# The end of a transformer layer: scattered parts added at once, the norm's gain multiplied in early, and its mean and bias added by two-row matrix products

## The chip, the core and the metric

The kernel runs on one core of one Trainium2 chip. The core has a matrix engine (TensorE, PE in the profile; its weight loads are listed as PEld), a vector engine (VectorE, DVE), an activation engine (ScalarE, ACT), a general engine (GpSimd, POOL) and an engine that only issues transfers (SyncE, SP). ACT can issue transfers as well. Sixteen DMA engines carry all transfers. The metric is the device time of one execution, in microseconds (us).

## What is computed

The reference is one layer of a diffusion transformer on 512 latent tokens of width 1024. The end of it is what matters here: a mixture of 16 experts, of which each takes its 64 best tokens, and then a layer norm.

```python
def ec_moe(h, w_router, b_router, w1, w3, w2):
    cap = EC_CAPACITY * n // N_EXPERTS                 # 64
    aff = softmax(h @ w_router + b_router)
    g, idx = lax.top_k(swapaxes(aff, 1, 2), cap)
    xe = h[bidx, idx]
    hid = silu(xe @ w1) * (xe @ w3)                    # per expert
    ye = (hid @ w2) * g[..., None]
    return zeros_like(h).at[bidx, idx].add(ye)

x = layer_norm(ALPHA * x + g2 * ec_moe(x * (1 + sc2) + sh2, *moe), ln2_g, ln2_b)

def layer_norm(x, g, b):
    return (x - mean(x)) * rsqrt(var(x) + EPS) * g + b
```

All arithmetic is float32. The weights w1, w3 and w2 of the sixteen experts are 201 MB and are read once.

## The kernel before

**Stages.** The first half of the kernel is attention and is untouched. From about 600 us on the experts run in eight pairs (`for pr in range(E_N // 2)`, L1232). The tokens are kept as four tiles of 128 rows, `xn[0]` to `xn[3]` (normalized input) and `acc[0]` to `acc[3]` (the running sum, four tiles of 128x1024).

**One pair.** `gather` builds 0/1 rows (`oh`) and multiplies them with `xn` on TensorE (L1137), which picks the 128 tokens of the pair. `up_` multiplies with w1 and w3 (L1174), `hid_t` transposes the result (L1182, copied by ACT in L1183), `down` multiplies with w2 (L1190), and `scatter` scales, splits into a high and a low part and adds the rows back into `acc` through TensorE (L1203, L1204). `gather` for pair 7, the last reader of `xn`, runs inside pair 6, between the two `hid_t` of that pair.

**Weights.** Each piece of 512 KB (`piece`, L957) is loaded by SP into a ring of 36 pages just ahead of its use. SP's instructions run in order. Each transfer from SP or ACT also takes one of eight completion semaphores in turn, and waits until the transfer that had it last has landed.

**The last pair.** Its w2 is cut by columns into three parts (`PARTS`, L40: columns 0 to 383, 384 to 767, 768 to 1023), in 16 pieces of 384 KB and 4 of 512 KB. L1308 multiplies a part into `py`; `put` then scales it (L1283, DVE), splits it (L74 on ACT, the high part; L77 on DVE, the low part), and its `rest` adds it back: for each row tile two products of TensorE (L1291), the addition on DVE (L1295) and the norm's statistics in blocks of 128 columns (L1297). For the third part the sum stays in PSUM (`fin[t]`, started by L1276 with `acc` itself). The code calls `rest` of a part only after the first pieces of the next one (L1310), so that TensorE multiplies while DVE and ACT split.

**The norm.** DVE merges the statistics (L1320), POOL adds epsilon and takes the power -0.5 (L1321, L1322), DVE makes minus mean times factor (L1323). Columns 768 to 1023 go ACT (L1325, from PSUM), POOL times gain (L1329), POOL plus bias (L1330), out. Columns 0 to 767 take two DVE instructions per row tile: (x - mean) times gain (L1335), times factor plus bias (L1336), out (L1337). The gain and bias, each spread over 128 partitions (512 KB), are loaded by SP behind the last weights (L1265).

**Order.** TensorE's instructions stay in written order (`manual_schedule`); a scheduler orders the others engine by engine.

Of the kernel before, what the change touches and what calls it, by code (L numbers as in the profile page):

```python
# [18 lines left out]
D = 1024  # L19
# [10 lines left out]
E_N = 16  # L30
# [21 lines left out]
def _layer(tc, A, out, opened):  # L52
# [1179 lines left out]
    for pr in range(E_N // 2):  # L1232
# [25 lines left out]
        waiting = py, ohT, gt  # L1258


    prefetch(len(order_r))
    ln2 = []
    for nm, place in (("ln2_g", "xe"), ("ln2_b", "hid")):
        b = me.tile([128, D], F32, name="ln2", tag=place, bufs=1)
        dma(b, A[nm].to_broadcast([128, D]))  # L1265
        ln2.append(b)
    lng, lnb = ln2
# [10 lines left out]
    def put(q, py):  # L1278
# [7 lines left out]
        def rest():  # L1286
            for t in range(NT):
# [8 lines left out]
                for b in range(0, w, BN_W):  # L1296
                    V.bn_stats(bs[:, t, (c0 + b) // BN_W, :], r[:, b:b + BN_W])  # L1297
        return rest

    rest = None  # L1300
    for q, (c0, w, ks) in enumerate(PARTS):
        py = psd.tile([128, 512], F32, name="y", bufs=2)
        for kh in range(KD // ks):
# [6 lines left out]
            if rest:  # L1310
                rest()
                rest = None
        rest = put(q, py)
    rest()
    order_.close()
    ov = out[0].rearrange("(t p) d -> p t d", p=128)
    mv = me.tile([128, NT, 2], F32, name="mv2")
    rs2 = me.tile([128, 2, NT], F32, name="rs2")
    for t in range(NT):
        V.bn_aggr(mv[:, t, :], bs[:, t])  # L1320
    G.tensor_scalar(rs2[:, 0, :], mv[:, :, 1], 1.0, EPS / ALPHA ** 2, op0=OP.mult, op1=OP.add)  # L1321
# [60 lines left out]
```

## Time and profile before

| | |
|---|---|
| median of 3 runs | 1049.84 us (1048.28 to 1052.63) |
| the profiled execution | 1047.56 us, of which the span is 1045.8 us |
| mean granted TensorE clock | 0.981 of full |
| TensorE, DVE, ACT, POOL busy | 977.7, 451.9, 278.2, 176.1 us (93, 43, 27, 17%) |
| chain that ended last | PE 72%, DMA 16%, DVE 7%, ACT 2%, issue 2%, POOL 2% |
| read from and written to HBM | 261.47 MB and 2.10 MB |

All times inside the kernel are from the start of the span. Busy shares are averages over a long first half that does not change; what the end of the layer is worth has to be read in the stretch from about 940 us on. A matrix product of float32 shows as two records of TensorE, and TensorE's busy time is modelled where products are pipelined.

### The profile page before, as it was taken

To read this page: it belongs to the slowest core of one execution; us is meant where nothing else is said; L and a number is where in the kernel's file an instruction comes from. 1 tells how busy PE (TensorE), PEld (TensorE's weight loads), DVE (VectorE), ACT (ScalarE), POOL (GpSimd) and SP (SyncE) were. 2 spreads that over 40 slices of the span, in tenths; PEclk is the share of its full clock that TensorE was granted. 3 is DMA by queue.
4 is the path that set the end of the run, shared out by engine and by line. 5 is a ranking of instruction groups with operands and counts; after the bars stand their busy time and mean duration, and the time that the engine had idled before them with its cause. 6 is when DMAs were issued, how large, how long until landed. Compare 5 with 4: busy or idle time off the path is not lost.

```text
span 1045.8 us, 13799 instructions
## 1 busy us (share of the span) xinstructions
PE 977.7 (93%) x5266; PEld 614.1 (59%) x5266; DVE 451.9 (43%) x870; ACT 278.2 (27%) x556; POOL 176.1 (17%) x177
## 2 busy tenths in 40 slices
PE   6999998989999999999986999999999999999992
PEld 5888976768778777777754443535353534334331
DVE  2382365753678556648473512221313131111227
ACT  1222324224777555544120101010101010010010
POOL 2340020202577422210020500000000000000004
PEclk9999999999999999999997999999999999999996
DMA  9944347763012000028948979999999999999993
GB/s 297 290 152 136 97 115 247 232 201 82 21 39 58 22 19 22 21 82 295 411 167 321 371 300 409 409 409 409 409 410 409 408 410 407 410 409 409 409 372 115
DMA packets 101209, 266.97 MB, mean 255 GB/s; under 512 B 14020, under 2 KB 37528, under 8 KB 101144
## 3 DMA queue, kind: packets, MB, share of 16 engines
q1 hardware_dynamic: 100248, 264.52, 68.3%
q0 software_dynamic: 320, 1.05, 0.4%
q8 instruction: 41, 0.67, 0.3%
q10 hardware_dynamic: 576, 0.52, 0.1%
q14 instruction: 24, 0.20, 0.1%
HBM read 261.47 MB, written 2.10 MB: 252 GB/s over the span
## 4 chain that ended last, share of the span: by engine, by line
PE 72%; DMA 16%; DVE 7%; ACT 2%; issue 2%; POOL 2%; SPq 0%; DVEq 0%; ACTq 0%; POOLq 0%
PE h L1174 16%; DMA wr<-moe_w 10%; PE y L1190 9%; PE mx L1137 6%; PE acc L83 5%; PE acc L82 5%; PE acc L81 5%; PE sc L652 4%; PE tpb L660 3%; DMA wa<-w_ada 3%; PE av L840 3%; PE mx L1203 2%; DMA wraw<-w_in 2%; PE tp L236 2%; PE po L83 1%
## 5 line engine op out<-in xcount | busy, mean ns | idle before, releaser
L1174 PE MATMUL h<-wr,xe 128*64 128x512 f32 x1024 | 233.6, 598 | 8.7 <-DMA wr<-moe_w 7.2
L1174 PEld LDWEIGHTS h<-wr,xe 128*64 128x64 f32 x1024 | 68.3, 136 | 162.9 <-issue 106.6
L1190 PE MATMUL y<-wr,hidT 128*64 128x512 f32 x448 | 97.7, 594 | 0.0
L641 DVE TENSOR_REDUCE nm<-sc 128x1 f32<-128x768 f32 x64 | 61.0, 953 | 34.3 <-PE sc L652 33.8
L1177 DVE TENSOR_TENSOR hid<-hid,h 128x512 f32<-128x512 f32 x16 | 11.0, 687 | 145.2 <-PE h L1174 145.2
L1149 POOL TENSOR_TENSOR oh<-oh,aff 128x512 f32<-128x512 f32 x8 | 8.4, 1048 | 352.8 <-PE mx L1137 352.8
L1190 PEld LDWEIGHTS y<-wr,hidT 128*64 128x64 f32 x448 | 31.5, 137 | 61.8 <-issue 58.1
L642 ACT ACTIVATE P<-sc,nm 128x768 f32<-128x768 f32 x64 | 57.6, 901 | 31.8 <-DVE nm L641 22.7
L1137 PE MATMUL mx<-oh,xn 128*128 128x128 f32 x512 | 60.3, 279 | 1.4 <-DVE oh L1127 1.4
L1137 PEld LDWEIGHTS mx<-oh,xn 128*128 128x128 f32 x512 | 59.2, 196 | 2.5 <-issue 1.3
L74 ACT ACTIVATE whi<-wraw 128x1024 fp32r<-128x1024 f32 (+1 forms) x32 | 33.5, 1046 | 99.4 <-DMA wraw<-w_in 75.4
L77 DVE TENSOR_TENSOR wlo<-wraw,whi 128x1024 fp32r<-128x1024 f32 (+1 forms) x32 | 39.2, 1227 | 45.2 <-PE acc L82 29.7
L74 ACT ACTIVATE ye<-y 128x512 fp32r<-128x512 f32 (+2 forms) x17 | 9.7, 572 | 178.8 <-DVE y L1197 98.7
L81 PE MATMUL acc<-xlh,whi 128*128 128x512 f32 x128 | 51.5, 402 | 2.1 <-ACT whi L74 2.1
L1204 DVE TENSOR_TENSOR acc<-acc,mx 128x512 f32<-128x512 f32 x56 | 34.7, 680 | 41.4 <-PE mx L1203 41.4
L1176 ACT ACTIVATE hid<-h 128x512 f32<-128x512 f32 x16 | 9.6, 597 | 155.6 <-PE h L1174 155.6
L82 PE MATMUL acc<-xll,whi 128*128 128x512 f32 x128 | 50.7, 396 | 0.0
L83 PE MATMUL acc<-xlh,wlo 128*128 128x512 f32 x128 | 50.2, 401 | 0.3 <-DVE wlo L77 0.3
L81 PE MATMUL acc<-whi,xlh 128*128 128x512 f32 (+1 forms) x128 | 49.6, 391 | 1.0 <-ACT whi L74 1.0
L1197 DVE SCALAR_TENSOR_TENSOR y<-y,gate,g2b 128x512 f32<-128x512 f32 x14 | 9.9, 754 | 92.5 <-PE y L1190 92.5
L83 PE MATMUL acc<-whi,xll 128*128 128x512 f32 (+1 forms) x128 | 48.7, 381 | 0.5 <-POOL xll L77 0.5
L82 PE MATMUL acc<-wlo,xlh 128*128 128x512 f32 (+1 forms) x128 | 48.8, 381 | 0.2 <-DVE wlo L77 0.2
(339 smaller groups left out, 1707.3 us busy)
## 6 DMA issues: line engine op xcount, KB each, us to landing
wr<-moe_w SPq DMA_DIRECT2D x372, 512.0 KB, 10.2
wa<-w_ada SPq DMA_DIRECT2D x32, 512.0 KB, 4.3
wraw<-w_in SPq DMA_DIRECT2D x28, 512.0 KB, 5.2
wa<-w_ada SPq DMA_DIRECT2D x8, 1024.0 KB, 9.4
wr<-moe_w SPq DMA_DIRECT2D x16, 384.0 KB, 8.5
outraw<-w_out SPq DMA_DIRECT2D x8, 512.0 KB, 9.6
xq<-x SPq DMA_DIRECT2D x4, 512.0 KB, 8.2
q<-q SPq DMA_DIRECT2D x16, 128.0 KB, 2.3
```

Of the source, the lines that this page charges most:

```text
L74: S.activation(hi, src, AF.Copy)
L77: (eng_lo or V).tensor_tensor(lo, src, f(hi), op=OP.subtract)
L81: T.matmul(ps, lh, rh, start=start, stop=False)
L82: T.matmul(ps, lh, rl, start=False, stop=False)
L83: T.matmul(ps, ll, rh, start=False, stop=stop)
L641: V.tensor_reduce(nm, ps[:, :768], axis=AX.X, op=OP.max, negate=True)
L642: S.activation(p, ps[:, :768], AF.Exp, bias=nm, accum_out=z)
L652: T.matmul(ps[:, a:b], l, r[:, a:b], start=i == 0, stop=i == len(passes) - 1)
L1137: T.matmul(pss[hf][:, kk * 128:(kk + 1) * 128], xn[t][:, k * 128:(k + 1) * 128], o[:, t].rearrange("p e s -> p (e s)"), start=t == 0, stop ...
L1174: T.matmul(ph[i][64 * hf:64 * hf + 64, :], xe[:, k, sl], w[:, hf * 512:(hf + 1) * 512], start=k == 0, stop=k == KD - 1)
L1190: T.matmul(py[hf][r0:r0 + 64, :], hT[:, e % 2, fc % 4, fc // 4, :], w[:, hf * 512:(hf + 1) * 512], start=fc == 0, stop=fc == KD - 1)
L1204: V.tensor_tensor(acc[t][:, hs], acc[t][:, hs], ps, op=OP.add)
```

## The change

- The gain and bias rows are loaded by ACT at the end of pair 6, into tiles of `xn` that have no reader any more: the two spread copies of 512 KB (into `xn[1]`, `xn[2]`), and both as two single rows of 4 KB (`gbr`, in `xn[0]`).
- `rest` of a part follows its `put` at once; nothing of the next part stands between.
- After the statistics of parts 0 and 1, each row tile is multiplied by the gain in place, by DVE for part 0 and POOL for part 1.
- Epsilon is added by DVE instead of POOL.
- Minus mean times factor and a column of ones (`mrs`) are transposed by TensorE (four small products into one PSUM tile), copied by DVE into a tile of two rows (`mr`), and multiplied with the gain and bias rows: the product is (-mean x factor) x gain + bias for a whole row tile, 512 and 256 columns at a time.
- Columns 0 to 767 then take one DVE instruction per product: x times factor plus the product, read from PSUM. The last row tile goes out in two transfers, the others in one.

```diff
+        if pr == E_N // 2 - 2:
+            lng, lnb, gbr = xn[1], xn[2], xn[0][0:2]
+            for i, nm in enumerate(("ln2_g", "ln2_b")):
+                S.dma_start(xn[1 + i], A[nm].to_broadcast([128, D]))
+                S.dma_start(xn[0][i:i + 1], A[nm])
...
-    for nm, place in (("ln2_g", "xe"), ("ln2_b", "hid")):
-        b = me.tile([128, D], F32, name="ln2", tag=place, bufs=1)
-        dma(b, A[nm].to_broadcast([128, D]))
...
                 for b in range(0, w, BN_W):
                     V.bn_stats(bs[:, t, (c0 + b) // BN_W, :], r[:, b:b + BN_W])
+                if not last:
+                    (G if q else V).tensor_tensor(r, r, lng[:, qs_], op=OP.mult)
...
-            if rest:
-                rest()
-                rest = None
-        rest = put(q, py)
-    rest()
+        put(q, py)()
...
-    G.tensor_scalar(rs2[:, 0, :], mv[:, :, 1], 1.0, EPS / ALPHA ** 2, op0=OP.mult, op1=OP.add)
-    G.tensor_tensor(rs2[:, 0, :], rs2[:, 0, :], negh[:, :NT], op=OP.pow)
-    V.scalar_tensor_tensor(rs2[:, 1, :], mv[:, :, 0], -1.0, rs2[:, 0, :], op0=OP.mult, op1=OP.mult)
+    V.tensor_scalar(rs2, mv[:, :, 1], EPS / ALPHA ** 2, None, op0=OP.add)
+    G.tensor_tensor(rs2, rs2, negh[:, :NT], op=OP.pow)
+    V.scalar_tensor_tensor(mrs[:, :, 0], mv[:, :, 0], -1.0, rs2, op0=OP.mult, op1=OP.mult)
+    mt = psd.tile([128, 512], F32, name="mx", bufs=3)
     for t in range(NT):
-        S.activation(acc[t][:, c0:], fin[t], AF.Identity, scale=rs2[:, 0, t:t + 1], bias=rs2[:, 1, t:t + 1])
+        T.transpose(mt[0:2, t * 128:(t + 1) * 128], mrs[:, t, :], ident)
+    mr = me.tile([2, 512], F32, name="mr", tag="hid", bufs=1)
+    V.tensor_copy(mr, mt[0:2])
+    for t in range(NT):
+        S.activation(acc[t][:, c0:], fin[t], AF.Identity, scale=rs2[:, t:t + 1], bias=mrs[:, t, 0:1])
+        G.tensor_tensor(acc[t][:, c0:], acc[t][:, c0:], lng[:, c0:], op=OP.mult)
+        G.tensor_tensor(acc[t][:, c0:], acc[t][:, c0:], lnb[:, c0:], op=OP.add)
+        S.dma_start(ov[:, t, c0:], acc[t][:, c0:])
     for t in range(NT):
         o = acc[t]
-        G.tensor_tensor(o[:, c0:], o[:, c0:], lng[:, c0:], op=OP.mult)
-        G.tensor_tensor(o[:, c0:], o[:, c0:], lnb[:, c0:], op=OP.add)
-        S.dma_start(ov[:, t, c0:], o[:, c0:])
-        parts = [slice(0, c0)] if t < NT - 1 else [slice(0, c0 // 2), slice(c0 // 2, c0)]
-        for p in parts:
-            V.scalar_tensor_tensor(o[:, p], o[:, p], mv[:, t, 0:1], lng[:, p], op0=OP.subtract, op1=OP.mult)
-            V.scalar_tensor_tensor(o[:, p], o[:, p], rs2[:, 0, t:t + 1], lnb[:, p], op0=OP.mult, op1=OP.add)
-            dma(ov[:, t, p], o[:, p])
+        for a, b in ((0, 512), (512, c0)):
+            w = psd.tile([128, 512], F32, name="y" if a else "mx", bufs=2 if a else 3)
+            T.matmul(w[:, :b - a], mr[:, t * 128:(t + 1) * 128], gbr[:, a:b], start=True, stop=True)
+            V.scalar_tensor_tensor(o[:, a:b], o[:, a:b], rs2[:, t:t + 1], w[:, :b - a], op0=OP.mult, op1=OP.add)
+            if t == NT - 1:
+                dma(ov[:, t, a:b], o[:, a:b])
+        if t < NT - 1:
+            dma(ov[:, t, :c0], o[:, :c0])
```

On ACT, at the end of pair 6 (`xn_4497` to `xn_4499` are `xn[0]` to `xn[2]`), the order before (-) and now (+) is:

```order
 L1176 ACTIVATE hid<-h 128x512
-L1183 ACTIVATE hidT<-mx 128x512 x2
+L1183 ACTIVATE hidT<-mx 128x512
+L1264 DMA xn_4497<-ln_g 1x1024
+L1183 ACTIVATE hidT<-mx 128x512
+L1263 DMA xn_4498<-ln_g 128x1024
+L1263 DMA xn_4499<-ln_b 128x1024
+L1264 DMA xn_4497<-ln_b 1x1024
 L74 ACTIVATE ye<-y 128x512 x2
```

The four loads stand there in the middle of the weights of the last two pairs; one of them stands ahead of the second copy of `hidT`.

On TensorE, in the last pair (L1308 has become L1311), the order before is:

```order
L1308 MATMUL y<-wr,hidT 64x384 x20
L1291 MATMUL mx<-ye,ohT 128x384 x8
L1308 MATMUL y<-wr,hidT 64x384 x12
L1308 MATMUL y<-wr,hidT 64x256 x8
L1291 MATMUL mx<-ye,ohT 128x384 x8
L1308 MATMUL y<-wr,hidT 64x256 x8
L1291 MATMUL h<-ye,ohT 128x256 x6
L1291 MATMUL mx<-ye,ohT 128x256 x2
```

and now, with the first of the four repeated groups at the end:

```order
L1311 MATMUL y<-wr,hidT 64x384 x16
L1291 MATMUL mx<-ye,ohT 128x384 x8
L1311 MATMUL y<-wr,hidT 64x384 x16
L1291 MATMUL mx<-ye,ohT 128x384 x8
L1311 MATMUL y<-wr,hidT 64x256 x16
L1291 MATMUL h<-ye,ohT 128x256 x6
L1291 MATMUL mx<-ye,ohT 128x256 x2
L1325 MATMUL mx<-ident,mrs 2x128 x4
L1338 MATMUL mx<-xn_4497,mr 128x512
L1338 MATMUL y<-xn_4497,mr 128x256
```

Each adding back now comes directly behind its own part, and twelve products follow where TensorE had nothing left.

On ACT, at the very end, the order before and now (L1325 has become L1330, L1331 has become L1333) is:

```order
-L1325 ACTIVATE acc<-h,rs_7704 128x256 x3
-L1325 ACTIVATE acc<-mx,rs_7704 128x256
-L1331 DMA out<-acc 128x256 x4
+L1330 ACTIVATE acc<-h,mrs,rs_7713 128x256 x3
+L1333 DMA out<-acc 128x256 x3
+L1330 ACTIVATE acc<-mx,mrs,rs_7713 128x256
+L1333 DMA out<-acc 128x256
```

The fourth ACTIVATE, which reads `fin[3]` and frees its PSUM tile, stands now behind three transfers that go out.

## Rows read from the trace of the kernel before

**Rows 1.** Windows: stretch, length, busy PE PEld DVE ACT POOL, clock, DMA share, GB/s.

```profile
760.00:800.00 40.00, 40.00 (x218) 18.94 (x216) 8.60 (x17) 2.99 (x5) 1.05 (x1) 1.00 1.03 409
...
1024.00:1026.00 2.00, 0.80 (x8) 0.27 (x4) 1.89 (x8) 0.01 (x1) 0.00 (x0) 1.00 0.00 0
```

**Rows 2.** Timeline, TensorE, pair 7: start, length, instructions, idle before, releaser.

```profile
989.69 1.08 PE L1174 MATMUL h<-wr,xe 128*64 128x512 f32 x4 [0.20 <-DMA wr<-moe_w]
```

**Rows 3.** DMA issues from 980 us: count, size, median us to landing.

```profile
wr<-moe_w SPq DMA_DIRECT2D x11, 512.0 KB, 10.2
...
ln<-ln_g SPq DMA_DIRECT2D x1, 512.0 KB, 8.7
```

**Rows 4.** Chain that ended last, two pieces near the end: start, length, what.

```profile
1009.41 9.24 DMA wr<-moe_w
...
1041.72 0.96 DVE acc L1336
```

**Rows 5.** Timeline, the last pair's parts, TensorE, DVE and ACT.

```profile
1007.28 0.51 PEld L1308 LDWEIGHTS y<-wr,hidT 128*64 128x64 f32 x5 [0.32 <-DMA wr<-moe_w]
...
1008.83 0.62 DVE L1283 SCALAR_TENSOR_TENSOR y<-y,gate,g2b 128x384 f32<-128x384 f32 x1 [8.30 <-PE y L1308]
...
1010.07 0.56 DVE L77 TENSOR_TENSOR ye<-y,ye 128x384 fp32r<-128x384 f32 x1 [0.62 <-ACT ye L74]
...
1010.83 0.98 PE L1291 MATMUL mx<-ye,ohT 128*128 128x384 f32 x4
...
1012.42 1.25 DVE L1297 BATCH_NORM_STATS2 oh<-acc 128x6 f32<-128x128 f32 x6
...
1013.11 4.85 PE L1308 MATMUL y<-wr,hidT 128*64 128x384 f32 x26
...
1022.85 1.95 PE L1308 MATMUL y<-wr,hidT 128*64 128x256 f32 x16
```

**Rows 6.** Timeline, the tail behind the last part.

```profile
1025.42 0.47 DVE L1283 SCALAR_TENSOR_TENSOR y<-y,gate,g2b 128x256 f32<-128x256 f32 x1
...
1028.90 1.04 DVE L1320 BATCH_NORM_AGGREGATE mv<-oh 128x2 f32<-128x48 f32 x4
...
1030.04 0.83 POOL L1321 TENSOR_SCALAR rs<-mv 128x4 f32<-128x4 f32 x1 [82.79 <-DVE mv L1320]
1030.95 1.04 POOL L1322 TENSOR_TENSOR rs<-rs,negh 128x4 f32<-128x4 f32 x1
1032.03 0.16 DVE L1323 SCALAR_TENSOR_TENSOR rs<-mv,rs 128x4 f32<-128x4 f32 x1 [1.22 <-POOL rs L1322]
```

**Rows 7.** Timeline, a form (busy, mean ns), one line (min/median/max ns): like operations.

```profile
999.66 0.66 PE L1182 MATMUL mx<-ident,hid 128*128 128x128 f32 x4
...
1001.08 1.46 PE L1276 MATMUL h<-acc,ident 128*128 128x256 f32 x6
...
L1308 PE MATMUL y<-wr,hidT 128*64 128x384 f32 x64 | 11.9, 493 | 0.2 <-DMA wr<-moe_w 0.2
...
L1197 DVE SCALAR_TENSOR_TENSOR y<-y,gate,g2b x14: 749/754/759, 621.7 to 961.1; 128x512 f32<-128x512 f32 x14
```

**Rows 8.** Timeline: POOL beside DVE that reads PSUM, and beside the tail's DVE.

```profile
141.49 5.73 POOL L315 TENSOR_TENSOR dq<-rt,rt 128x256 f32<-128x256 f32 x8 [13.02 <-DVE rt L312]
...
1036.57 1.32 POOL L1330 TENSOR_TENSOR acc<-acc,ln 128x256 f32<-128x256 f32 x1
```

**Rows 9.** Windows: length, PE busy, clock, DMA share, GB/s; the last as in Rows 1.

```profile
176.50:177.00 0.50, 0.50 (x2) 0.50 0.00 0
...
179.50:180.00 0.50, 0.50 (x5) 0.99 0.73 107
...
212.00:212.50 0.50, 0.00 (x0) 1.00 0.43 172
...
213.50:214.00 0.50, 0.50 (x4) 0.65 0.72 213
...
1029.25:1029.50 0.25, 0.00 (x0) 0.00 (x0) 0.25 (x3) 0.00 (x0) 0.00 (x0) 0.86 0.00 0
```

More of the change, by code (lines that the diff above doesn't have):

```diff
@@ L1258, in _layer @@
         waiting = py, ohT, gt
-    prefetch(len(order_r))
-    ln2 = []
-    for nm, place in (("ln2_g", "xe"), ("ln2_b", "hid")):
-        b = me.tile([128, D], F32, name="ln2", tag=place, bufs=1)
-        dma(b, A[nm].to_broadcast([128, D]))
-        ln2.append(b)
-    lng, lnb = ln2
+        if pr == E_N // 2 - 2:
[3 more added lines that the diff above has]
+                S.dma_start(xn[0][i:i + 1], A[nm])
+    prefetch(len(order_r))
     nb = D // BN_W
@@ L1297, in rest @@
                     V.bn_stats(bs[:, t, (c0 + b) // BN_W, :], r[:, b:b + BN_W])
-        return rest
-    rest = None
+                if not last:
+                    (G if q else V).tensor_tensor(r, r, lng[:, qs_], op=OP.mult)
+        return rest
+    mrs = me.tile([128, NT, 2], F32, name="mrs")
+    V.memset(mrs[:, :, 1], 1.0)
     for q, (c0, w, ks) in enumerate(PARTS):
@@ L1309, in _layer @@
                              start=fc == 0, stop=fc == KD - 1)
-            if rest:
-                rest()
-                rest = None
-        rest = put(q, py)
-    rest()
-    order_.close()
+        put(q, py)()
     ov = out[0].rearrange("(t p) d -> p t d", p=128)
     mv = me.tile([128, NT, 2], F32, name="mv2")
-    rs2 = me.tile([128, 2, NT], F32, name="rs2")
+    rs2 = me.tile([128, NT], F32, name="rs2")
     for t in range(NT):
         V.bn_aggr(mv[:, t, :], bs[:, t])
-    G.tensor_scalar(rs2[:, 0, :], mv[:, :, 1], 1.0, EPS / ALPHA ** 2, op0=OP.mult, op1=OP.add)
@@ L1326, in _layer @@
-    done = []
+        T.transpose(mt[0:2, t * 128:(t + 1) * 128], mrs[:, t, :], ident)
[6 more added lines that the diff above has]
+        S.dma_start(ov[:, t, c0:], acc[t][:, c0:])
@@ L1327, in _layer @@
     for t in range(NT):
         o = acc[t]
-        G.tensor_tensor(o[:, c0:], o[:, c0:], lng[:, c0:], op=OP.mult)
-        G.tensor_tensor(o[:, c0:], o[:, c0:], lnb[:, c0:], op=OP.add)
-        S.dma_start(ov[:, t, c0:], o[:, c0:])
-        parts = [slice(0, c0)] if t < NT - 1 else [slice(0, c0 // 2), slice(c0 // 2, c0)]
-        for p in parts:
-            with tc.issue_after(done[-1].ins) if t > 1 else nullcontext():
-                V.scalar_tensor_tensor(o[:, p], o[:, p], mv[:, t, 0:1], lng[:, p], op0=OP.subtract, op1=OP.mult)
-            done.append(V.scalar_tensor_tensor(o[:, p], o[:, p], rs2[:, 0, t:t + 1], lnb[:, p], op0=OP.mult, op1=OP.add))
-            dma(ov[:, t, p], o[:, p])
+        for a, b in ((0, 512), (512, c0)):
[4 more added lines that the diff above has]
+                dma(ov[:, t, a:b], o[:, a:b])
@@ L1340 @@
+        if t < NT - 1:
+            dma(ov[:, t, :c0], o[:, :c0])
+    order_.close()
 _INS = ["x", "c", "ctx", "c_ctx", "w_ada", "b_ada", "w_in", "mla_g_q", "mla_w_uq", "mla_g_kv", "mla_w_ukv",
```

## The prediction

> **What bounds the kernel now.** I read the windows first. From 640 us on the sixteen DMA engines are busy all the time and deliver 409 GB/s; nothing moves any more from 1024 us [rows 1]. So the experts run at the pace of their weights. The timeline says the same from TensorE's side: in pair 7 it works 1.08 us and then waits 0.20 us for the next piece [rows 2], and a piece of 0.524 MB takes 1.28 us at 409 GB/s. In the chain of waits the weights hold the end until 1018.65 us (1009.41 + 9.24) [rows 4]. Then a different stage begins: add part 2 back, norm, write. It runs from the scaling of part 2, at 1025.42 us [rows 6], to the end of the span at 1045.8 us, 20.4 us, and DVE is last (1041.72 + 0.96 = 1042.68 us [rows 4]), 3.1 us before the end. So there are three terms: A, what delays the weights; B, the way from part 0's scaling to part 2's; C, these 20.4 us.
>
> **A, the loads.** Two transfers of 0.524 MB leave a place behind the last weights, where they cost nothing: the one of the gain took 8.7 us to land in a queue that had only weights ahead of it [rows 3], and the norm that needs it came later. Now they stand among the weights of pairs 6 and 7, and there the engines have no gap [rows 1]. 1.049 MB at 409 GB/s is 2.56 us, by which every later weight lands later. TensorE is ahead of the weights (0.20 us per piece), so it passes the delay on: up to part 0 all shifts by 2.6 us. Bounds: 0, if the stream had room that the share does not show, and 2.6, since they are the same bytes.
>
> The waits that come with it: ACT's first load waits for the end of `gather` in pair 6. Behind it on ACT stands the second copy of `hidT`, which needs products that come after the same `gather`, so nothing is lost. SP shares the eight semaphores with these loads, and its transfers queue behind a load that is still out; with transfers that take 10.2 us to land at 1.28 us a piece [rows 3], eight are under way, which feeds the engines for some 10 us, and the loads' own bytes for 2.6 more. SP would have to be held longer than that. I take no gap.
>
> **B, adding back at once.** From L1283 of part 0 to the low part is 1.80 us (1008.83 to 1010.63) [rows 5]. Adding back takes 2.28 us from its first product at 1010.83 to the next part's first at 1013.11 [rows 5], of which the first 0.28 is the high part, which now starts before the low one is ready. So part 1 starts 1.80 + 2.0 = 3.8 us after L1283. It has 16 pairs of records; 13 pairs took 4.85 us [rows 5], in which the length of the last record, 0.49 [rows 7], counts once: 0.33 a pair, and 16 pairs with that end 5.4 to 5.8; I take 5.4, since the 13 had a wait at their end. Part 2's eight pairs took 1.95 [rows 5]; with an end of 0.4 that is 0.2 a pair and 3.6 for 16. Sum from L1283 of part 0 to that of part 2: 3.8 + 5.4 + 3.8 + 3.6 = 16.6 us, and 0.1 for the two steps to DVE; before it was 1025.42 - 1008.83 = 16.6. **B is 0.1.** What TensorE lost before in waits for weights (0.32 us at 1007.28 [rows 5], and more at the start of part 2) it now loses in waits for DVE and ACT, and since part 0 was finished by its last weight, A passes through whole. DVE has 12 statistics there at 0.21 and four additions, and now four multiplications, at no more than L77's 0.56 [rows 5]: 7.0 us at most. From the first product put back to part 1's scaling lie 3.8 - 1.8 + 5.4 = 7.4, so they are hidden, though barely; what they need beyond that would make part 1's scaling late by as much. POOL's four, about 1.1 each by the columns of [rows 8], lie in time in which it is idle. The fill of `mrs` and the two small rows are there long before they are read.
>
> Each adding back leaves TensorE idle for 1.24 us (1008.83 to 1010.07 [rows 5]), with small gaps after. The clock can fall in such a place: it was 1.00 at 212.00 us, with TensorE idle, and 0.65, on its way to 0.50, at 213.50 when TensorE worked again [rows 9]. It did not fall when TensorE stopped at 1024.80 [rows 5] for the wait behind part 2 [rows 1]. I take no fall; each would cost some 1.5 us (half of a stretch at 1.2 GHz like that from 176.50 to 179.50 [rows 9]), so B reaches from -0.5 (DVE, busy with part 1, held part 2's scaling by about that before) to 3.1.
>
> **C, the tail, counted from L1283 of part 2.** The merged statistics end at +4.5 as before (1028.90 + 1.04) [rows 6]. Epsilon on DVE costs 0.16, by L1323, plus a step, instead of POOL's 0.83 and its step; the power keeps its 1.04 [rows 6]. So the factor is there 0.75 us earlier, and the transposes start at +6.1. What comes next is new:
>
> - Four transposes took 0.66 at full clock [rows 7], 0.13 a piece and the end of the last. With TensorE idle the clock fell at 1029.25 [rows 9], +3.9 in this count: here they find 1.2 GHz. Twice 0.13 a piece and a longer end: 1.05, so +7.15.
> - The copy of two rows of 512 out of PSUM: 0.75 at most, by L1197, which reads PSUM too [rows 7]; +7.9.
> - The products. Six records of 256 columns take 1.46, less 0.16 that the last one is longer [rows 7]: 0.216 a record, two records a product. So 256 columns cost 0.43, 512 cost 0.86, a row tile 1.29 at 2.4 GHz and 2.57 at 1.2. Four row tiles: 5.15 or 10.3.
> - DVE from PSUM: 0.75 for 512 columns [rows 7], 0.47 for 256 [rows 6], 1.2 a row tile. So TensorE is the slower, at either clock.
>
> Which clock: at 176.50 us TensorE worked without a gap at 0.50, and the 1.00 came at 179.50 [rows 9], 3 us later; I take the same here, +7.9 to +11. That does 1.55 us of the 5.15; the other 3.6 end at +14.6, with the last record's end +15.0. DVE's last two instructions end at +15.85. The 3.1 us behind DVE's end stay: +18.95. **C is 18.95 - 20.4 = -1.4.** Bounds: all at 2.4 GHz, +17.5, -2.9; all at 1.2 GHz, +22.1, +1.7.
>
> POOL's eight operations beside: DVE that reads PSUM left POOL at 5.73 / 8 = 0.72 each, the tail of before had 1.32 [rows 8]. From ACT's start at +6.1 they end near +13.6, fourth row tile included, before DVE.
>
> **The sum.** 2.6 + 0.1 - 1.4 = +1.3 us on the profiled execution's 1047.56: 1048.9. That execution lies 2.3 us below the median of its runs, 1049.84; the forecast for the median is 1051.1.
>
> **Rivals.**
>
> 1. The products stay at 1.2 GHz. Place: from +7.9 on. For it: the clock is down when they start [rows 9], and each waits for a PSUM tile that DVE or ACT must free. Against: at half clock TensorE takes 2.57 a row tile and DVE 1.2, so it finds the tiles free and has no gap. Price: C = +1.7, the sum +4.4, **1054.2**: slower than before. The change loses from the point where the low clock takes more than the first 0.5 us of the products; with one fall in B besides it is 1055.7. The Trainium skill, TensorE: Matmul & The Clock Gate, section A second HAM failure mode: psum-queue depth-cycling, says that a TensorE which idles for moments between groups of products while it cycles through PSUM banks goes back and forth between the clocks. By that rule this rival holds; no row here shows such a cycle.
> 2. The weights absorb the loads: A = 0, **1048.5**. For it: only that the loads come while TensorE is behind, after `gather`. Against: the engines, not TensorE, are full there [rows 1].
> 3. The last row tile hangs on POOL. ACT's fourth ACTIVATE, which frees the PSUM tile for the fourth product of 512, stands behind three transfers, and the third waits for POOL's sixth operation: +11.1 at 0.72 each, and the product wants its tile at +13.5, so it is free. If POOL runs at 1.32, as in the old tail [rows 8], it is +14.7, the tile comes at about +15.6 behind the transfer's issue and ACT, and the end moves out by 2: **1053.1**. From 1.0 an operation on it decides. Against: DVE reads PSUM in the new tail, as it did beside the 0.72.
> 4. The products run at full clock throughout: C = -2.9, **1049.6**.
>
> On A there is a rule that speaks against the change. The Trainium skill, DMA: Bandwidth & Descriptors, section Issuing engines are not separate DMA queues, says that transfers from ACT and SP end on the same sixteen engines and interleave. By it, another queue hides nothing and A is whole; with a queue of its own, the sum would be rival 2's. No row here shows both queues at work on a full stream.
>
> **How the numbers follow.** The forecast has 0.5 (1050 to 1052.5), rival 1 0.18, rival 2 0.1, rival 3 0.12, rival 4 0.1. The range reaches from below rival 2 to rival 1, and a little further on either side for the runs of before, which alone spread from 1048.28 to 1052.63: 1047.3 to 1054.8. Half a per cent, about what a measurement of this kernel can tell from no change, is 5.2 us. For faster by that, A would have to be 0 and C beyond its bound: 0.03. For slower, rival 1 with a fall in B: 0.09. Within: 0.88.
>
> **What would show it.** The DMA share stays at 1.03 through the loads, and L1283 of part 0 comes 2.6 us later than 1008.83; if it does not, A is wrong. L1283 of part 2 comes 16.6 us behind it, at a clock of 1.00; 18 or more means a fall. The transposes start 6.1 us behind that, the products show 0.86 and then 0.43 a record of 512 columns, DVE is last at about +15.9, and POOL's operations take 0.72. Wrong would be the forecast if the factor took as long as before, if the products' records are longer than a like product's, or if a gap opens in the weights where SP waits for a load.

## The result and the profile after

The changed kernel takes 1056.34 us (median of 12 runs, 1053.25 to 1060.62), the kernel before 1049.30 us beside it (12 runs, 1044.16 to 1052.63). The ratio is 1.0074 with a 95% interval of 1.0057 to 1.0091: slower by 7.8 us (6.0 to 9.5) by the ratio, which is not that of the medians; +1.3 was forecast. The time lies above the top of the range, 1054.8.

The profiled execution took 1058.75 us, its span is 1056.9. I cut it at the three places of the prediction. A runs from the first product of the last gather (L1137, pair 7) to L1283 of part 0, B from there to L1283 of part 2, C from there to the end of the span. The timeline of the changed kernel, TensorE and DVE, at these places (start, length, instruction, idle time before it and what ended it):

```profile
940.75 0.94 PE L1137 MATMUL mx<-oh,xn 128*128 128x128 f32 x7
...
1015.17 0.62 DVE L1283 SCALAR_TENSOR_TENSOR y<-y,gate,g2b 128x384 f32<-128x384 f32 x1 [8.17 <-PE y L1311]
...
1034.90 0.49 DVE L1283 SCALAR_TENSOR_TENSOR y<-y,gate,g2b 128x256 f32<-128x256 f32 x1 [1.73 <-PE y L1311]
```

So A is 1015.17 - 940.75 = 74.4 us, B 19.7 and C 1056.9 - 1034.90 = 22.0. In the profile of before the same places are at 938.75, 1008.83 [rows 5], 1025.42 [rows 6] and 1045.8: A 70.1, B 16.6, C 20.4. The difference of the spans, 11.1 us, is 4.3 in A, 3.1 in B, 1.6 in C, and 2.0 before the last gather, in code that the change doesn't touch. That start moves by itself: over the sixteen profiles below it lies between 935.7 and 942.6 us, in no order with their edits. The forecast for the three terms was 2.6, 0.1 and -1.4.

**In A the transfers slow down.** Windows of the changed kernel around the new loads (columns as in [rows 1]; the last two are DMA share and GB/s). Where [rows 1] had 1.03 and 409, there are now twenty microseconds with less, the last five (960 to 965) at 0.95 and 374:

```profile
940.00:945.00 5.00, 5.00 (x45) 4.74 (x43) 1.16 (x3) 0.60 (x1) 0.00 (x0) 1.00 1.03 411
945.00:950.00 5.00, 5.00 (x40) 3.89 (x40) 2.26 (x7) 0.60 (x1) 1.05 (x1) 1.00 0.94 347
950.00:955.00 5.00, 5.00 (x26) 1.65 (x24) 0.00 (x0) 0.00 (x0) 0.00 (x0) 1.00 1.02 346
955.00:960.00 5.00, 4.99 (x24) 1.26 (x20) 0.00 (x0) 0.00 (x0) 0.00 (x0) 1.00 0.97 364
```

SP's queue is held by the new loads too. Its waits between 930 and 975 us (total us, times, longest us):

```profile
SPq L938 <- DMA xn<-ln_g: 6.3, 2, 5.6
SPq L938 <- DMA xn<-ln_b: 1.6, 1, 1.6
```

**In B the clock falls twice.** First the products that add a part back, in TensorE's timeline, then the windows around them (the clock is third from the end):

```profile
1016.43 1.38 PE L1291 MATMUL mx<-ye,ohT 128*128 128x384 f32 x4 [1.30 <-ACT ye L74]
...
1018.11 1.65 PE L1291 MATMUL mx<-ye,ohT 128*128 128x384 f32 x4 [0.30 <-DVE acc L1295]
...
1027.42 3.56 PE L1291 MATMUL mx<-ye,ohT 128*128 128x384 f32 x8 [1.60 <-ACT ye L74]
```

```profile
1018.00:1020.00 2.00, 1.89 (x6) 1.44 (x8) 2.00 (x9) 0.00 (x0) 0.00 (x0) 0.50 1.05 369
1020.00:1022.00 2.00, 2.00 (x10) 0.76 (x8) 2.00 (x7) 0.00 (x0) 0.00 (x0) 0.69 1.10 354
1022.00:1024.00 2.00, 2.00 (x14) 0.84 (x12) 1.74 (x6) 0.00 (x0) 0.00 (x0) 1.00 1.10 349
1028.00:1030.00 2.00, 1.98 (x5) 1.33 (x6) 1.19 (x3) 0.00 (x0) 0.00 (x0) 0.52 0.00 0
1030.00:1032.00 2.00, 2.00 (x12) 1.23 (x12) 2.00 (x9) 0.00 (x0) 1.42 (x2) 0.63 0.00 0
1032.00:1034.00 2.00, 2.00 (x22) 1.28 (x20) 1.17 (x6) 0.00 (x0) 1.87 (x3) 1.00 0.00 0
```

The four products from 1018.11 take 1.65 us; the like four in e9 below, at a clock of 1.00, take 1.08. (The 1.38 of the first four is not the clock's, which is still 1.00 up to 1017.6; e9 has 1.39 there: the low half of `ye` is ready only at 1016.97.) In both parts TensorE waits for the halves of `ye`, 1.30 and 1.60 us, and the clock is at 0.50 shortly behind it: the lower level, 1.2 GHz, of two.

**In C the products run at 1.2 GHz to the end.** TensorE, then the windows:

```profile
1041.02 1.01 PE L1325 MATMUL mx<-ident,mrs 128*2 128x128 f32 x4 [3.54 <-DVE mrs L1321]
1042.81 2.07 PE L1338 MATMUL mx<-xn,mr 2*128 2x512 f32 x2 [0.77 <-DVE mr L1327]
1044.67 1.06 PE L1338 MATMUL y<-xn,mr 2*128 2x256 f32 x2
1045.53 1.91 PE L1338 MATMUL mx<-xn,mr 2*128 2x512 f32 x2
...
1048.09 1.91 PE L1338 MATMUL mx<-xn,mr 2*128 2x512 f32 x2
```

```profile
1044.00:1050.00 6.00, 6.00 (x11) 3.01 (x10) 2.45 (x4) 0.56 (x1) 3.55 (x5) 0.50 0.42 151
1050.00:1053.00 3.00, 3.00 (x6) 1.46 (x5) 1.63 (x3) 0.00 (x0) 0.00 (x0) 0.50 0.59 232
```

TensorE works without a gap for nine microseconds, and the clock does not come back. The first product starts 7.9 us behind L1283 of part 2 and the transposes 6.1 us behind it, both as forecast. A row tile then takes 2.56 us (1045.53 to 1048.09), as the forecast had it for 1.2 GHz, and the span ends at +22.0, on the forecast's bound for 1.2 GHz throughout, +22.1.

### The profile page after: what moved, and what is told of

It is laid out like the page before. It is cut to its first block, busy times and chain, and to the rows that moved or that the text cites. A ratio compares the mean times of both kernels' runs of the same rounds, so it can differ in the third digit from the quotient of the medians.

```text
span 1056.9 us, 13844 instructions
## 1 busy us (share of the span) xinstructions
PE 995.2 (94%) x5286; PEld 623.0 (59%) x5286; DVE 448.3 (42%) x875; ACT 278.2 (26%) x556; POOL 174.6 (17%) x180
## 4 chain that ended last, share of the span: by engine, by line
PE 76%; DMA 14%; DVE 5%; ACT 2%; issue 1%; POOL 1%; SPq 0%; DVEq 0%; ACTq 0%; POOLq 0%
PE h L1174 15%; DMA wr<-moe_w 10%; PE y L1190 8%; PE acc L83 6%; PE acc L82 6%; PE acc L81 6%; PE mx L1137 6%; PE sc L652 5%; PE tpb L660 3%; PE av L840 2%; PE mx L1203 2%; PE av L776 2%; PE y L1311 1%; DMA wa<-w_ada 1%; PE tp L236 1%; PE po L83 1%
## 5 line engine op out<-in xcount | busy, mean ns | idle before, releaser
L1137 PE MATMUL mx<-oh,xn 128*128 128x128 f32 x512 | 60.7, 280 | 1.4 <-DVE oh L1127 1.4
L1137 PEld LDWEIGHTS mx<-oh,xn 128*128 128x128 f32 x512 | 59.6, 197 | 2.5 <-issue 1.3
## 6 DMA issues: line engine op xcount, KB each, us to landing
wr<-moe_w SPq DMA_DIRECT2D x372, 512.0 KB, 10.2
```

The costliest lines, as they stand in the source:

```text
L1137: T.matmul(pss[hf][:, kk * 128:(kk + 1) * 128], xn[t][:, k * 128:(k + 1) * 128], o[:, t].rearrange("p e s -> p (e s)"), start=t == 0, stop ...
```

## The experiments

Each kernel gives a ratio to the kernel before and, from its one profile, the three terms, read at the places shown above. Differences of time in microseconds are a ratio less one, times 1049. The terms are of one execution, and the time is of all of them: the sum of a kernel's three terms, less that of before, lies in the interval of its time in ten of the fifteen kernels, and outside it in e3, e6, e9, e10 and e11. The profiled execution is the fastest of its kernel's runs in e1, e6 and e7, the slowest in e5 and e13. So the terms tell where time goes, and a difference of time is called shown only where its interval says so.

| kernel | A | B | C | ratio (95% interval) |
|---|---|---|---|---|
| before | 70.1 | 16.6 | 20.4 | 1 |
| changed | 74.4 | 19.7 | 22.0 | 1.0074 (1.0057 to 1.0091) |
| e1, broadcast loads early | 72.7 | 16.6 | 20.9 | 1.0032 (1.0016 to 1.0047) |
| e2, an eighth of their bytes | 70.9 | 16.6 | 20.6 | 1.0004 (0.9991 to 1.0018) |
| e10, one-row loads early | 69.8 | 16.6 | 20.8 | 1.0020 (1.0004 to 1.0036) |
| e13, all four loads early | 74.5 | 16.6 | 20.2 | 1.0028 (1.0014 to 1.0043) |
| e9, changed, one-row loads late | 73.2 | 17.1 | 22.3 | 1.0088 (1.0071 to 1.0106) |
| e3, changed, rest held back | 75.4 | 16.6 | 22.0 | 1.0037 (1.0023 to 1.0050) |
| e4, changed, products in the waits | 74.6 | 17.4 | 22.0 | 1.0068 (1.0045 to 1.0091) |
| e5, changed, products of 128 rows | 74.7 | 19.9 | 20.4 | 1.0080 (1.0058 to 1.0101) |
| e6, changed, busy before the tail | 74.5 | 18.7 | 21.3 | 1.0105 (1.0084 to 1.0126) |
| e11, as e6, scalings first | 74.8 | 19.8 | 18.8 | 1.0038 (1.0017 to 1.0058) |
| e7, tail and gain alone | 69.9 | 19.0 | 22.0 | 1.0046 (1.0028 to 1.0065) |
| e12, as e7, 128 rows, held busy | 70.0 | 18.9 | 18.5 | 1.0007 (0.9987 to 1.0028) |
| e8, as e7, one pass | 70.2 | 19.0 | 17.6 | 1.0003 (0.9986 to 1.0020) |
| e14, as e8, gain on POOL | 69.9 | 16.6 | 17.9 | 0.9975 (0.9960 to 0.9991) |

### The loads (A)

e1 is the kernel before with the two broadcast loads moved:

```diff
+        if pr == E_N // 2 - 2:
+            lng, lnb = xn[1], xn[2]
+            for i, nm in enumerate(("ln2_g", "ln2_b")):
+                S.dma_start(xn[1 + i], A[nm].to_broadcast([128, D]))
```

(and without SP's loads behind the last weights).

> The kernel before with one thing changed: gain and bias (two broadcast loads of 512 KB) are issued by ACT at the end of pair 6 into xn[1] and xn[2], as in the change, and no longer by SP behind the last weights. The row loads, the multiplications, the order of adding back and the tail are those of before. Theory 1 (the two loads alone make the whole of the later arrival of the weights): from the start of the last gather to L1283 of part 0 the trace shows 74.4 us instead of 70.1, the stretch from there to L1283 of part 2 stays at 16.6, and the time is 1049.3 + 4.3 = 1053.6 us. Theory 2 (the loads cost only their bytes, 2.56 us, and the rest comes from the two one-row loads of 4 KB): 72.6 us, and the time 1051.9.

A is 72.7, 2.6 us more than before: the bytes, and nothing else. Time +3.4 us (1.7 to 4.9). e2 fills 16 partitions in place of 128:

```diff
-                S.dma_start(xn[1 + i], A[nm].to_broadcast([128, D]))
+                S.dma_start(xn[1 + i][:16], A[nm].to_broadcast([16, D]))
```

> As the run before it, but each of the two loads fills 16 of the 128 partitions (64 KB instead of 512 KB); the other 112 partitions of gain and bias are left as they were, so the output lacks the right gain and bias there. Where and how they are issued, and what waits for them, is the same. Theory 1 (beyond its bytes a load costs because SP's queue of weights is held until it lands): bytes 2.56 / 8 = 0.3 and the hold 1.7, so 70.1 + 2.0 = 72.1 us from the gather to L1283 of part 0, time 1051.3. Theory 2 (all of the cost goes with the bytes, moved more slowly than the weights): 70.1 + 4.3 / 8 = 70.6 us, time 1049.8.

A is 70.9, 0.8 more than before, 0.3 of it the bytes; the time does not differ. The waits of SP's queue in e1, then in e2, between 930 and 975 and between 925 and 975 us:

```profile
SPq L938 <- DMA xn<-ln_g: 6.0, 1, 6.0
SPq L938 <- DMA xn<-ln_b: 1.6, 1, 1.6
```

```profile
SPq L938 <- DMA xn<-ln_g: 4.0, 1, 4.0
...
SPq L938 <- DMA xn<-ln_b: 0.5, 1, 0.5
```

In e1 SP is held for 7.6 us, as long as in the changed kernel within 0.3, and A grows by the bytes alone; in e2 a hold of 4.5 us costs 0.5 beyond the bytes. So these waits are not the difference between e1 and the changed kernel. What the changed kernel has besides are the two one-row loads. e10 adds only them to the kernel before, e13 all four loads, and e9 takes the one-row loads out of the changed kernel's place and puts them behind the last weights:

```diff
 # e10: behind pair 6, the kernel before otherwise
+            for i, nm in enumerate(("ln2_g", "ln2_b")):
+                S.dma_start(xn[0][i:i + 1], A[nm])
 # e9: behind prefetch(len(order_r)), the changed kernel otherwise
+    for i, nm in enumerate(("ln2_g", "ln2_b")):
+        dma(xn[0][i:i + 1], A[nm])
```

> The kernel before with only the two one-row loads (4 KB each, into xn[0], read by nobody) issued by ACT at the end of pair 6; its own loads of gain and bias stay with SP behind the last weights. Theory 1 (a one-row load costs by itself, whatever goes beside it): 70.1 + 1.7 = 71.8 us or more from the gather to L1283 of part 0, time 1051. Theory 2 (it costs only beside the broadcast loads, in the same queue): 70.1, time 1049.3.

> The changed kernel with the two one-row loads (4 KB each, gain and bias into xn[0]) issued by SP behind the last weights; the two broadcast loads stay with ACT at the end of pair 6, and all else stays. Theory 1 (the one-row loads are what takes the stretch from the gather to L1283 of part 0 from the 72.7 us of the kernel with the broadcasts alone to the 74.4 of the change): 72.7, time 1056.3 - 1.7 = 1054.6. Theory 2 (it is something else of the change): 74.4 or more, time 1056.3.

> The kernel before with the whole of the change's edit of the loads and nothing else: both broadcasts and both one-row loads by ACT at the end of pair 6 (the rows are read by nobody). Theory 1 (the one-row loads cost 1.5 to 2 us beside the broadcasts, though they cost nothing alone): 74.3 to 74.8 us from the gather to L1283 of part 0, time 1049.0 + 4.4 = 1053.4. Theory 2 (the loads cost the 2.6 us of their bytes, and the rest of the change's 4.3 comes from elsewhere in it): 72.7 us, time 1051.6.

By the profiles the one-row loads cost only in company: 69.8 alone, 72.7 for the broadcasts alone, 74.5 for both, and 74.4 to 75.4 in all six other kernels that have both; without them, late, 73.2. The windows show where. e1, then e13, the first ten microseconds behind the new loads (in e13 there are 0.98 and 354 from 960 to 965 as well):

```profile
945.00:950.00 5.00, 5.00 (x26) 1.70 (x24) 0.00 (x0) 0.00 (x0) 0.00 (x0) 1.00 1.00 398
950.00:955.00 5.00, 5.00 (x26) 1.50 (x24) 0.00 (x0) 0.00 (x0) 0.00 (x0) 1.00 0.99 374
```

```profile
950.00:955.00 5.00, 5.00 (x27) 1.69 (x27) 1.25 (x4) 0.60 (x1) 1.03 (x1) 1.00 0.96 338
955.00:960.00 5.00, 5.00 (x26) 1.71 (x24) 0.00 (x0) 0.00 (x0) 0.00 (x0) 1.00 0.95 366
```

The times are too coarse to confirm the 1.8 us: e10 is +2.1 us (0.4 to 3.7) with no longer A, e13 (+2.9 us, 1.5 to 4.5) and e1 do not differ, and e9 is no faster than the changed kernel, with a gather that starts late in its profile, at 942.35.

The traces also show what a row of 4 KB takes: not bytes, but a turn. Each of ACT's loads has one of the eight semaphores in turn, and SP's pieces pass it over. SP's pieces in the ten microseconds from 3 us before to 7 us behind the start of the last gather, in the kernel before, e1 and the changed kernel (line, instruction, count, duration in ns, first and last start):

```profile
L938 SPq DMA_DIRECT2D wr<-moe_w x8: 327/328/583, 936.0 to 945.0; - x8
L938 SPq DMA_DIRECT2D wr<-moe_w x6: 328/328/473, 932.9 to 941.9; - x6
L938 SPq DMA_DIRECT2D wr<-moe_w x4: 327/327/328, 938.0 to 945.7; - x4
```

Eight pieces are issued there before, six where ACT has two loads (e1, and e2, e9 and e10), four where it has four (the changed kernel, e3, e4, e5, e6, e11 and e13). So when the loads start, nearly 7 us into the gather, fewer pieces are under way: the last two issued there take 10.2 us to land before and 6.3 in the changed kernel. From 6 to 9 us into the gather, before the bytes of the broadcasts come, the engines' share is 1.02 at 403 GB/s in e1 and 0.87 at 318 in the changed kernel. That six pieces under way nearly feed the engines, and four do not, fits A in all of these kernels, e10 included; no run changes the number of turns by itself, so it is read from the traces and not tested.

### Adding back at once (B)

e3 holds the rest of a part back behind half of the next part's products, as the kernel before did; e4 leaves the order and gives TensorE products that nobody reads:

```diff
 # e3
-        put(q, py)()
+            if rest:
+                rest()
+                rest = None
+        rest = put(q, py)
 # e4
-        put(q, py)()
+        rest = put(q, py)
+        if q < len(PARTS) - 1:
+            du = psd.tile([128, 512], F32, name="y", bufs=2)
+            for n in (512, 256):
+                T.matmul(du[:, :n], ident, xn[3][:, :n], start=True, stop=True)
+        rest()
```

> The changed kernel with one thing undone: the rest of a part (products into the rows, sums, statistics, gain) is held back behind half of the next part's products, as before. Loads, multiplications and tail are those of the change. Theory 1 (the waits of adding back at once are what let the clock fall between L1283 of part 0 and of part 2): that stretch goes from 19.7 back to 16.6 us at a granted clock of 1.00, the other two stay at 74.4 and 22.0, time 1056.3 - 3.1 = 1053.2. Theory 2 (the multiplications by the gain on DVE and POOL are what slows it): it stays at 19 us or more, time 1056.

> The changed kernel with products added whose results nobody reads: behind the last weight product of part 0 and of part 1, in the wait for the halves of ye, TensorE does one product of 512 and one of 256 columns (ident with xn[3]). Nothing else is changed. Theory 1 (the fall of the clock is what costs; the waits by themselves do not): the clock stays at 1.00 through both parts, L1283 of part 0 to L1283 of part 2 takes 16.7 us instead of 19.7, time 1053.3. Theory 2 (the waits themselves cost the 3 us): the stretch stays at 19.7 or gets longer whatever the clock is, time 1056.3 or more.

With the rest held back B is 16.6 again, with all of the change's multiplications in it, and the time falls to +3.9 us (2.4 to 5.2); the terms of its profile, with A at 75.4, would give 6.9. With products in the waits B is 17.4, and the clock stays at the upper level through both parts (e4's windows):

```profile
1012.00:1022.00 10.00, 9.55 (x49) 4.28 (x45) 7.42 (x22) 0.49 (x1) 0.00 (x0) 1.00 1.08 362
1022.00:1031.00 9.00, 7.64 (x46) 4.15 (x44) 5.94 (x19) 0.67 (x2) 3.93 (x4) 1.00 0.16 52
```

So of the 3.1 us the falls make 2.4 and the waits 0.8. The kernels that have the change's own code for B fit: e9's profile shows no fall and B of 17.1, e6's one fall and 18.7, those of the changed kernel, e5 and e11 two falls each and 19.7 to 19.9, so a fall costs some 1.2 to 1.3 us. That is seven falls in ten waits of the same code: whether the clock falls differs from profile to profile. The time of e4, +7.1 us (4.7 to 9.5), does not show the 2.4 us; its interval reaches to within 0.7 us of the 4.0 that theory 1 gave.

### The tail (C)

e5 makes the eight products over 128 rows, 126 of them zeros:

```diff
-            lng, lnb, gbr = xn[1], xn[2], xn[0][0:2]
+            lng, lnb, gbr = xn[1], xn[2], xn[0]
+    mr = me.tile([128, 512], F32, name="mr", tag="hid", bufs=1)
+    G.memset(mr, 0.0)
-    mr = me.tile([2, 512], F32, name="mr", tag="hid", bufs=1)
-    V.tensor_copy(mr, mt[0:2])
+    V.tensor_copy(mr[0:2], mt[0:2])
```

> The changed kernel with the tail's eight products made over 128 rows instead of two: mr has 128 rows, zero but for its first two (POOL clears it beforehand), and gbr is the whole of xn[0], whose other rows are finite and meet the zeros. The columns, the waits and everything else are those of the change. Theory 1 (the clock stays down in the tail because a product of two rows works on two of 128 rows): the clock rises while the products run, one product of 512 columns gets shorter on the way, and L1283 of part 2 to the end takes 19 to 20.5 us instead of 22.0, time 1054 to 1055. Theory 2 (the rows are not what counts): granted clock 0.50 to the end, 22.0 us, time 1056.3.

C is 20.4, in theory 1's range. In TensorE's timeline of e5 the products get shorter on the way; the windows have the clock:

```profile
1045.24 2.05 PE L1339 MATMUL mx<-xn,mr 128*128 128x512 f32 x2 [0.86 <-DVE mr L1328]
...
1047.93 1.91 PE L1339 MATMUL mx<-xn,mr 128*128 128x512 f32 x2
...
1052.12 1.02 PE L1339 MATMUL mx<-xn,mr 128*128 128x512 f32 x2
```

```profile
1050.00:1051.00 1.00, 1.00 (x3) 0.67 (x2) 0.90 (x2) 0.00 (x0) 0.92 (x2) 0.50 0.79 307
1051.00:1052.00 1.00, 1.00 (x4) 0.47 (x3) 0.32 (x2) 0.00 (x0) 0.12 (x1) 0.92 0.01 3
1052.00:1053.00 1.00, 1.00 (x5) 0.50 (x4) 1.00 (x2) 0.00 (x0) 0.00 (x0) 1.00 1.04 389
```

The clock came back 5.9 us after the first product (1045.24 to about 1051.2). In the five kernels with this tail of two rows, starting at 1.2 GHz (the changed one, e3, e4, e7, e9), it did not in ten. e5's return of the clock stands on one profile. The time, +8.4 us (6.1 to 10.6), does not show the 1.6 us.

The other way round: is a clock that is up held by products of two rows? e6 keeps TensorE busy until the transposes:

```diff
+    du = psd.tile([128, 512], F32, name="y", bufs=2)
+    for n in range(4):
+        T.matmul(du, ident, xn[3][:, :512], start=True, stop=True)
     mt = psd.tile([128, 512], F32, name="mx", bufs=3)
```

> The changed kernel with four products of 512 columns over 128 rows (ident with xn[3], read by nobody) between the last adding back and the transposes, where TensorE has nothing to do for 3.6 us; the waits of the parts before stay as in the change. Theory 1 (the two-row products by themselves cannot hold the clock): it falls to 0.50 while they run, and L1283 of part 2 to the end takes between 19 and 22 us. Theory 2 (the clock, once held through the wait, stays up in the two-row products): 1.00 to the end, and 17.5 us, time 1056.3 - 4.5 = 1051.8.

It told nothing on that. The first products ran at the full clock, and so fast that the third of 512 columns had to wait for the bank that ACT's fourth ACTIVATE frees: the mechanism of the prediction's rival 3, one product earlier than it said. TensorE's waits between 1038 and 1052 us:

```profile
PE mx L1341 <- ACT acc L1333: 2.0, 1, 2.0
```

The clock fell some 0.4 us into that wait, and whether the wait or the products before it let it fall can't be read here. Its profiled execution also has the lowest time of its runs (1055.38; they reach 1062.40), so its ratio and its terms don't belong together. e11 takes the wait away by putting the four ACTIVATEs ahead of the four DMAs:

```diff
     for t in range(NT):
         S.activation(acc[t][:, c0:], fin[t], AF.Identity, scale=rs2[:, t:t + 1], bias=mrs[:, t, 0:1])
+    for t in range(NT):
         G.tensor_tensor(acc[t][:, c0:], acc[t][:, c0:], lng[:, c0:], op=OP.mult)
```

> The changed kernel with the four products that keep TensorE busy before the transposes (read by nobody), and with ACT's four scalings ahead of its four DMAs, so that no product waits for the bank of the fourth scaling. Theory 1 (two-row products do not hold the clock even where TensorE has no gap): granted clock 0.50 from some point inside the products on, L1283 of part 2 to the end 19 to 21.5 us. Theory 2 (it was the wait of 2.0 us for the fourth scaling that let the clock fall in the run without this order): 1.00 until the last product, and 17.5 us.

```profile
1044.00:1046.00 2.00, 2.00 (x7) 0.96 (x7) 1.12 (x2) 0.31 (x1) 1.92 (x4) 1.00 0.20 66
1046.00:1047.00 1.00, 1.00 (x4) 0.53 (x3) 0.85 (x3) 0.00 (x0) 1.00 (x3) 0.80 0.04 15
1047.00:1050.00 3.00, 3.00 (x6) 1.67 (x5) 1.54 (x3) 0.00 (x0) 1.76 (x3) 0.50 1.01 378
```

The windows of e11: the clock falls at about 1046.6, with TensorE busy all of the time since 1043.72. Theory 1, though C is 18.8, below its 19 to 21.5: four of the eight products were done by then. The time is +4.0 us (1.8 to 6.1).

e7 leaves loads and order as they were before and has the tail and the gain alone; e12 adds to it products of 128 rows, the ACTIVATEs first, and the four products of e6:

```diff
 # e7: the changed kernel, rest held back as in e3, and behind prefetch(len(order_r))
+    lng, lnb, gbr = xn[1], xn[2], xn[0][0:2]
+    for i, nm in enumerate(("ln2_g", "ln2_b")):
+        dma(xn[1 + i], A[nm].to_broadcast([128, D]))
+        dma(xn[0][i:i + 1], A[nm])
```

> The kernel before with the tail of the change and its multiplication by the gain part by part, and nothing else of it: gain, bias and the two rows are loaded by SP behind the last weights (into xn), and the rest of a part is held back as before. Theory 1 (loads, clock in the parts, and tail each cost by themselves): 70.1 us from the gather to L1283 of part 0, 16.6 to L1283 of part 2, 22.0 from there to the end, time 1049.3 + 1.6 = 1050.9. Theory 2 (the multiplications by the gain delay the parts too, since they wait for a gain that lands after the weights): 16.6 becomes 18 or more, time 1052.5 or more.

> The tail and gain alone (loads by SP behind the weights, the rest of a part held back), with products of 128 rows, ACT's scalings ahead of its DMAs, and four products of 512 columns that nobody reads in the wait before the transposes. Theory 1 (128 rows without a wait hold the clock): granted clock 1.00 until the last product, L1283 of part 2 to the end 17.5 us, time 1049.3 - 2.9 = 1046.4. Theory 2 (the clock falls in the tail all the same, or DVE and the outputs hold the end): 19 us or more, time 1048 or more.

A and C of e7 came out at 69.9 and 22.0 as theory 1 said. B did not: 19.0, theory 2, at a clock of 1.00; the time, +4.8 us (2.9 to 6.8), has the sum of the two terms, 2.4 + 1.7, in its interval. e12, with the same B, kept 1.00 through all its products:

```profile
1037.00:1042.00 5.00, 5.00 (x16) 2.86 (x16) 3.48 (x7) 0.00 (x0) 3.71 (x6) 1.00 0.54 198
```

Between e11 and e12 the wait ahead of the products is alike (0.77 and 0.82 us), and so is their order; the rows are 2 and 128. The loads and the order of the parts differ too, but TensorE's work from the unread products on does not. C of e12 is 18.5, not 17.5: its unread products began at 1.2 GHz, took 4.58 us and held the transposes back by 1.4 (they start at +7.5 instead of +6.1).

### A kernel that beats both

What e7 loses in B stands in DVE's timeline. Its gain, issued behind the last weights at 1012.6 us, takes 8.8 us to land, and the four multiplications of part 0 come only behind that, ahead of the last six statistics and L1281, which is L1283 there:

```profile
1022.80 2.46 DVE L1297 TENSOR_TENSOR acc<-acc,xn 128x384 f32<-128x384 f32 x4
...
1026.35 0.47 DVE L1281 SCALAR_TENSOR_TENSOR y<-y,gate,g2b 128x256 f32<-128x256 f32 x1
```

e8 is e7 with products of one pass and the ACTIVATEs first; e14 gives POOL all of the gain:

```diff
 # e8
+    gbs = me.tile([2, D], F32R, name="gbs", tag="xe", bufs=1)
+    S.activation(gbs, gbr, AF.Copy)
-    mr = me.tile([2, 512], F32, name="mr", tag="hid", bufs=1)
+    mr = me.tile([2, 512], F32R, name="mr", tag="hid", bufs=1)
 # e14
-                    (G if q else V).tensor_tensor(r, r, lng[:, qs_], op=OP.mult)
+                    G.tensor_tensor(r, r, lng[:, qs_], op=OP.mult)
```

> The run before it with two more edits: mr and the rows of gain and bias are of type float32r, so that TensorE makes each of the eight products in one pass, and ACT does its four scalings one behind the other ahead of its four DMAs, as it did in the kernel before. Theory 1 (the products are the bound of the tail): what is left is DVE's 4 x (0.75 + 0.48) = 4.9 us behind the first product, the last DVE operation ends some 13.6 us after L1283 of part 2 instead of 19.0, and that stretch ends at 16.6 us instead of 22.0, time 1049.3 - 3.8 = 1045.5. Theory 2 (DVE, POOL or the outputs hold the tail as much as the products): 20 us or more, time 1049 or more.

> The kernel of the one-pass tail with one more edit: the multiplications by the gain are POOL's in part 0 as well, so that DVE has none of them. Theory 1 (the 2.4 us that this tail's kernels lost between L1283 of part 0 and of part 2 are DVE's four multiplications of part 0, 2.5 us, which stand ahead of L1283 of part 2): 16.6 us again, 17.6 from there to the end, time 1049.0 - 2.6 = 1046.4, faster than both kernels. Theory 2 (POOL with eight multiplications slows DVE or holds the factor back): 18 us or more, or 19 and more in the tail, time 1049 or more.

In e8 C fell to 17.6; a product of 512 columns was one record of 0.62 to 0.76 us at the same low clock, where it had been two of together 1.9. It is not the 16.6 expected, since now the outputs bound the end: DVE is done at 1041.5 us, and to 1044 the DMA engines are full (e8's windows):

```profile
1039.00:1041.00 2.00, 0.99 (x2) 0.28 (x1) 2.00 (x5) 0.00 (x0) 1.95 (x3) 0.50 0.98 371
1041.00:1044.00 3.00, 0.00 (x0) 0.00 (x0) 0.50 (x2) 0.00 (x0) 0.00 (x0) 0.50 1.00 371
```

In e8 the gain in C and the loss in B cancel (-2.7 and +2.4). e14 has B of 16.6 as well, and 1045.72 us against 1048.87: ratio 0.9975 (0.9960 to 0.9991), by which it is 2.6 us faster than the kernel before (0.9 to 4.2) and some 10 faster than the changed one. DVE's late multiplications were the 2.4 us (in e3, where the gain is there early, the same four lie between part 0's statistics and B is 16.6), and POOL does its eight without harm (of POOL, by form, 1010 to 1035 us):

```profile
L1297 POOL TENSOR_TENSOR acc<-acc,xn 128x384 f32<-128x384 f32 x8 | 7.7, 996 | 75.5 <-DVE oh L1295 75.5
```

## Why the prediction was wrong, point by point

**A, 2.6 forecast, 4.3 in the profile.** The bytes were right: the broadcasts alone make 2.6 (e1). The failed step is "I take no gap", and the term that was left out are the two one-row loads, which the sum priced at nothing; beside the broadcasts they make some 1.8 us in the profiles (74.5 in e13 against 72.7 in e1), and nothing alone (69.8 in e10, though its time is +2.1 us). The step counted on eight pieces under way to feed the engines while SP is held. With two loads six were left, and the waits of 7.6 us cost nothing more (e1); with four loads four were left, and the engines had gaps even before the bytes of the broadcasts came (share 0.87 from 946.75 to 949.75 us). That the turns are the reason is read from the traces. The Trainium skill, DMA: Bandwidth & Descriptors, section Issuing engines are not separate DMA queues, says that transfers started by either engine interleave on the same sixteen; the trace agrees: the broadcasts in ACT's queue cost the weights all of their bytes (A 72.7 in e1 against 70.1).

**B, 0.1 forecast, 3.1 in the profile.** The step that failed is "I take no fall". The row that I trusted, a clock that did not fall for the wait behind part 2, was one execution's wait; behind parts 0 and 1 five profiles of the same code now have a fall for seven of ten waits. Two falls, 2.4 us together, and 0.8 of waits make the 3.1, the upper bound given. The order of the work, 16.6 without falls, was sized nearly right: 17.1 where the clock stayed up by itself (e9), 17.4 where it was held (e4).

**C, -1.4 forecast, +1.6 in the profile.** Up to the first product every step came as worked out: factor, transposes at +6.1, product at +7.9. The failed step is "3 us later; I take the same here". The row behind it [rows 9] was of products over many rows. Products of two rows did not bring the clock back in ten microseconds, and did not hold it either (e11); of 128 rows they brought it back, after 5.9 us instead of 3 (e5). Rival 1 is what happened, at its price; with a fall in B it stood at 1055.7. Its mechanism is another than that of the Trainium skill's rule, TensorE: Matmul & The Clock Gate, section A second HAM failure mode: psum-queue depth-cycling, beside it: the trace has no idling between the products and no clock that goes to and fro, but one that stays down. Rival 3 needed faster products than the changed kernel has: there POOL took 0.72 us as forecast, and the bank was free in time; in e6 it was not.

**The sum.** +4.3, +3.1 and +1.6 are 9.0 us in one profile; the ratio of all runs gives +7.8. Each of the three steps lay at or beyond its bad bound, and the forecast had treated them as independent and unlikely; two of the three are the clock, and both times the choice was for the clock that the sum needed.

## What to carry to other kernels

Give a new wait on TensorE the price of a fall of the clock as a chance, unless rows show many such waits without one: here, for waits of 1.3 and 1.6 us, it was seven in ten at some 1.2 us each. Products of a few rows that start at the lower clock are best priced at it throughout; making each in one pass (float32r, 0.6 to 0.8 us for 512 columns against 1.9) gave a shorter tail here (17.6 us) than anything done for the clock (18.5 at best). A load that lands early is paid for in bytes wherever the engines are full, and, by these traces, where it shares turns with the stream, by a place in it whatever its size; one that lands late can hold up the work that needs it (e7). An edit that trades one for the other has to win that back elsewhere.

## What the runs showed of the hardware that was not expected

- Products of two rows that keep TensorE busy without a gap leave the granted clock at 0.50 for ten microseconds, and let it fall from 1.00 (at 1046.6 us in e11, 2.9 us after the first of them); the same products over 128 rows, mostly zeros, held 1.00 (e12) and brought it back from 0.50 in 5.9 us (e5). e5, e11 and e12 are one profile each.
- Two loads of one row of 4 KB each cost nothing alone (A 69.8 against 70.1), and some 1.8 us beside two broadcast loads in the same queue (74.5 against 72.7), with the DMA share at 0.95 to 0.98 instead of 0.99 to 1.02. SP had four pieces issued in ten microseconds with all four loads, six with two, eight with none; that this is the cause is read from the traces, not tested.
- SP, held for 7.6 us in two waits, lost nothing beyond the bytes of the loads that it waited for in e1 (A +2.6 us); in e2, held for 4.5 us, 0.5.
